# Delta-rule recurrence: inverses merged by 64 x 64 blocks in opposite corners of the array, chunk products kept for the second direction, decays built from stacked rows

## The chip, the cores and the metric

The kernel runs on one core of a Trainium2 chip. The metric is the device time in microseconds, from the launch of the program to its end, of that core. TensorE is called PE in the profile, VectorE DVE, ScalarE ACT, GpSimd POOL and SyncE SP.

## The reference, cut to what matters

The whole program is a two-layer block (two feed-forward networks and a mixer per layer) and then one block with a gated delta rule, a pooling mixer, and an expert-choice feed-forward network. Only the gated delta rule is changed. For each of 4 heads and two directions (forwards, and the sequence reversed) it computes, in chunks:

```python
g = cumsum(log_a)                                   # within a chunk
decay = where(i >= j, exp(g[i] - g[j]), 0)
m = where(i > j, (k*beta) @ k.T * decay, 0)
t_inv = inverse(eye + m)                            # unit lower triangular
w_blk = t_inv @ (k*beta*exp(g));  u_blk = t_inv @ (v*beta)
qk = (q @ k.T) * decay
# scan over the chunks, state s per head and direction:
u_new = u_n - w_n @ s
o_n = (q*exp(g)) @ s + qk @ u_new
s = s * exp(g_last) + (k*exp(g_last - g)).T @ u_new
```

It is computed twice: once for a context of 256 tokens, of which only the final states are wanted (no q), and once for the 512 tokens of the main sequence, which starts from those states.

## The kernel before, in words

The kernel takes chunks of 128 tokens, so the context has 2 and the main sequence 4. A *round* takes one chunk for each direction: round r has chunk r for the forward direction (d = 0) and the last chunk but r for the backward one (d = 1). So the main sequence has 4 rounds and the context 2, and each chunk is met twice, once by each direction. With 4 heads a round has 8 matrices of 128 x 128, m = 4 d + h.

`delta_gates` computes the decays' sums once. `delta_round` is one round up to the inverses, `delta_scan` (L1027) the rest of it. The steps of `delta_round` are:

- *decays*: per direction, two 512-column matmuls (L933, L934) and, for each head, three 128-column ones (L938) whose stationary operands are three parts of the log decay and whose moving operand is a triangle; then exp on ACT (L941) and a product on DVE (L942);
- *chunk products*: keys by keys per direction (L949), times the decays on DVE (L951) and with the diagonal taken out on POOL (L952); the 8 matrices Q go to a scratch tensor in DRAM (L957). In the main sequence also queries by keys (L966, L968);
- *blocks of 16*: the diagonal 16 x 16 blocks are read back, inverted row by row on DVE (L988, L989), and written to two other scratch tensors (L994), which hold zeros elsewhere; these are read back as T and U, 8 whole 128 x 128 matrices each (L999, L1000);
- *merges*: three levels that join blocks of 16, 32 and 64. Each level forms W from Q and T (L1009, copied to SBUF by ACT at L1010), then from W and U the new part of U (L1017) and, in two of the levels, that of T (L1022); a predicated copy on DVE puts the new quarter-blocks in their places (L1023, L1024).

Numbers are fp32; a product of two fp32 operands appears as two rows of 128 columns in the profile, one fp32r product as one row.

The context's rounds run one after the other as side work of the last feed-forward network of layer 1 (`ffn`, whose matmuls are L68 to L70): it takes two steps of the side work after each of its groups of matmuls. The main sequence's rounds are side work of `token_mixer`: its projections of q and v, its pooling mixer (L227 to L229, L1275, L1276, L1285) and its gate projection take 1 to 3 steps after each piece, and a `side.drain()` runs what is left. Two rounds may be open at a time, but a round reads T and U only when the round before has its U (`free`). After the drain the outputs are normalised (L1304 to L1314), turned (L1322) and go through the output projection (`mixer_out`, L68 to L70 again). The instructions are put in order on each engine when the program is built, so parts of the output projection can stand ahead of the last merges; each engine then keeps that order.

Of the kernel before, what the change touches and what calls it, by code (L numbers as in the profile page):

```python
# [11 lines left out]
F32 = mybir.dt.float32  # L12
# [807 lines left out]
def delta_gates(g, ab, nt, pool, pre):  # L820

    nc = g.nc

    def t(n):
        return pool.tile([128, nt, 8], F32, name=pre + n, bufs=1)

    r = {}
    u, la = t("gu"), t("la")
    nc.vector.tensor_add(u, ab[:, :, 0:8], bc(g.V2["dt_bias"][:, None, :], [128, nt, 8]))
    softplus(g, la, u, pool)  # L830
    nc.vector.tensor_mul(la, la, bc(g.V2["negA"][:, None, :], [128, nt, 8]))

    nc.vector.tensor_scalar(la, la, -127.0, None, op0=OP.max)
    be = t("be")
    nc.scalar.activation(be, ab[:, :, 8:16], AF.Exp, scale=-1.0)
    nc.vector.tensor_scalar(be, be, 1.0, None, op0=OP.add)
    nc.vector.reciprocal(be, be)

    a, rest = t("a"), t("rest")
    nc.vector.tensor_scalar(a, la, -786432.0, None, op0=OP.add)  # L840
    nc.vector.tensor_scalar(a, a, 786432.0, None, op0=OP.add)
    nc.vector.tensor_sub(rest, la, a)
    r["parts"] = [pool.tile([128, nt, 8], F32R, name=pre + n, bufs=1) for n in ("pa", "pb", "pc", "pn")]
    nc.vector.tensor_copy(r["parts"][0], a)
    split(g, r["parts"][1], r["parts"][2], rest)
    nc.vector.tensor_scalar(r["parts"][3], a, -1.0, None, op0=OP.mult)
    p = sm(g)
    pv = p[:, :32 * nt].rearrange("p (s a c h) -> p s a c h", s=2, a=2, h=8)
    for i, src in enumerate((a, rest)):
        for d, tri in ((0, g.triu), (1, g.tril)):  # L850
            nc.tensor.matmul(pv[:, 0, i, :, 4 * d:4 * d + 4], tri, src[:, :, 4 * d:4 * d + 4], start=True, stop=True)
        nc.tensor.matmul(pv[:, 1, i], g.ones, src, start=True, stop=True)
    sums = pool.tile([128, 2, 2, nt, 8], F32, name=pre + "sums", bufs=1)
    nc.vector.tensor_copy(sums, pv)

    ex = pool.tile([128, 4, nt, 8], F32, name=pre + "gex", bufs=1)
    nc.vector.tensor_add(ex[:, 0], sums[:, 0, 0], sums[:, 0, 1])
    nc.vector.tensor_sub(sums[:, 0], sums[:, 1], sums[:, 0])
    nc.vector.tensor_add(ex[:, 1], sums[:, 0, 0], sums[:, 0, 1])
    nc.vector.tensor_add(ex[:, 2], sums[:, 1, 0], sums[:, 1, 1])  # L860
    nc.vector.tensor_sub(ex[:, 3], sums[:, 0, 1], sums[:, 1, 1])
    nc.scalar.activation(ex, ex, AF.Exp)
    r["etot"], r["eg"] = ex[:, 2], ex[:, 0]
    r["neg_eg"], r["beta"], r["nbeta"], r["btail"] = t("neg"), t("bex"), t("nbe"), t("bt")
    nc.vector.tensor_scalar(r["neg_eg"], ex[:, 0], -1.0, None, op0=OP.mult)
    nc.vector.tensor_mul(r["btail"], be, ex[:, 1])
    nc.vector.tensor_mul(r["beta"], be, ex[:, 3])
    nc.vector.tensor_scalar(r["nbeta"], r["beta"], -1.0, None, op0=OP.mult)
    r["tri"], r["id"] = g.tri_r, g.id_r
    return r  # L870
# [53 lines left out]
def delta_round(g, cs, kf, gates, P, out, q=None):  # L924
# [4 lines left out]
    e = P["e"]()  # L929
    for d, (tri, mask) in enumerate(gates["tri"]):  # L930
        p = sm(g)
        pa, pb, pc, pn = [t[:, cs[d], 4 * d:4 * d + 4] for t in gates["parts"]]
        nc.tensor.matmul(hv(p), tri, bc(pn[:, :, None], [128, 4, 128]), start=True, stop=False, skip_group_check=True)  # L933
        nc.tensor.matmul(hv(p), gates["id"], bc(mask[:, None, :], [128, 4, 128]), start=False, stop=False,  # L934
                         skip_group_check=True)
        for h in range(4):
            for t in (pa, pb, pc):
                nc.tensor.matmul(p[:, h * 128:(h + 1) * 128], bc(t[:, h:h + 1], [128, 128]), tri, start=False,  # L938
                                 stop=t is pc, skip_group_check=True)
        ed = e[:, 4 * d:4 * d + 4, :]  # L940
        nc.scalar.activation(ed, hv(p), AF.Exp)  # L941
        nc.vector.tensor_mul(ed, ed, bc(gates["nbeta"][:, cs[d], 4 * d:4 * d + 4][:, :, None], [128, 4, 128]))  # L942
        yield
    Q = P["q"]()
    for d in range(2):
        p = sm(g)
        for h in range(4):
            hs = slice(h * 128, (h + 1) * 128)
            nc.tensor.matmul(p[:, hs], kf[cs[d]][:, hs], kf[cs[d]][:, hs], start=True, stop=True)  # L949
        Qd, ed = Q[:, 4 * d:4 * d + 4, :], e[:, 4 * d:4 * d + 4, :]  # L950
        nc.vector.tensor_mul(Qd, ed, hv(p))  # L951
        nc.gpsimd.tensor_mul(Qd, Qd, bc(g.offd[:, None, :], [128, 4, 128]))  # L952
        yield
# [4 lines left out]
    if q is not None:  # L958
        while len(q) < 4:
            yield  # L960
        at = P["at"]()
        for d in range(2):
            p = sm(g)
            for h in range(4):
                hs = slice(h * 128, (h + 1) * 128)
                nc.tensor.matmul(p[:, hs], kf[cs[d]][:, hs], q[h][:, cs[d] * 128:(cs[d] + 1) * 128],  # L966
                                 start=True, stop=True)
            nc.vector.tensor_mul(at[:, 4 * d:4 * d + 4, :], e[:, 4 * d:4 * d + 4, :], hv(p))  # L968
            yield
        out["at"] = at  # L970
# [24 lines left out]
    yield  # L995
    while not P["free"]():
        yield
    T, U = P["t"](), P["u"]()
    nc.sync.dma_start(T, matrices(scr[1]))  # L999
    nc.sync.dma_start(U, matrices(scr[2]))  # L1000
    yield

    for lev in range(3):
        W = P["w"]()
        for d in range(2):
            p = sm(g)
            for h in range(4):
                m = 4 * d + h
                nc.tensor.matmul(p[:, h * 128:(h + 1) * 128], Q[:, m, :], T[:, m, :], start=True, stop=True)  # L1009
            nc.scalar.copy(W[:, 4 * d:4 * d + 4, :], hv(p))  # L1010
        yield
        for d in range(2):
            ds = slice(4 * d, 4 * d + 4)
            pu = sm(g)
            for h in range(4):
                m = 4 * d + h
                nc.tensor.matmul(pu[:, h * 128:(h + 1) * 128], W[:, m, :], U[:, m, :], start=True, stop=True)  # L1017
            if lev < 2:
                p = sm(g)
                for h in range(4):  # L1020
                    m = 4 * d + h
                    nc.tensor.matmul(p[:, h * 128:(h + 1) * 128], U[:, m, :], W[:, m, :], start=True, stop=True)  # L1022
                nc.vector.copy_predicated(T[:, ds, :], bc(g.mrg[:, lev, d, :][:, None, :], [128, 4, 128]), hv(p))  # L1023
            nc.vector.copy_predicated(U[:, ds, :], bc(g.mrg[:, lev, 1 - d, :][:, None, :], [128, 4, 128]), hv(pu))  # L1024
            yield
    out["u"] = U


# [119 lines left out]
def token_mixer(g, I):  # L1148
# [40 lines left out]
    try:  # L1189
        while True:  # L1190
# [10 lines left out]

    spare = [[t, s, t] for t, s in zip([P.tile([128, S], F32, name=f"t_s{d}") for d in range(2)], st)]
    mem.update(at=lambda: P.tile([128, 8, 128], F32, name="t_at", bufs=2),
               u=lambda: P.tile([128, 8, 128], F32, name="t_u", bufs=2), s=lambda d: spare[d].pop())
    res = [{} for _ in range(NT)]
    chunks = [(r, NT - 1 - r) for r in range(NT)]

# [398 lines left out]
def constants():  # L1606
# [17 lines left out]
        "eye16": np.broadcast_to(np.eye(16).reshape(1, 256), (128, 256)),  # L1624
    }
    mrg = []
    for b in (16, 32, 64):
        low = (pc // (2 * b) == q // (2 * b)) & (pc % (2 * b) >= b) & (q % (2 * b) < b)
        mrg += [low, low.T]
    parts["mrg"] = np.concatenate(mrg, 1)  # L1630
    late = ("tril", "mnegb", "offd", "iota", "eye16", "mrg")
    cst, at = [], []
    for names in ([n for n in parts if n not in late], late):
        cst.append(np.ascontiguousarray(np.concatenate([parts[n].astype(np.float32) for n in names], 1)))
# [159 lines left out]
def spread(g, I):  # L1794
# [30 lines left out]
    for i in range(2):  # L1825
        ts = [g.dram.tile([1, 8 * CS], F32, name=f"ds{i}{j}") for j in range(3)]
        for t in ts[1:]:
            for m in (0, 4):
                nc.gpsimd.dma_start(matrices(t)[:, m:m + 4], z)
        g.dscr.append(ts)  # L1830


def setup2(g, I, C):

    g.w_in2 = I["w_in2"]
    _, at, _ = constants()
    cst = C.tile(list(I["cst2"].shape), F32, name="cst2")
    g.nc.scalar.dma_start(cst, I["cst2"])
    for n, sl in at[1].items():
        setattr(g, n, cst[:, sl])  # L1840
    g.mrg = g.mrg.bitcast(I32).rearrange("p (l d c) -> p l d c", l=3, d=2)
    g.s0 = [C.tile([128, S], F32, name=f"s0{d}") for d in range(2)]
    g.wr = C.tile([128, NK, 16], F32, name="wr")
    g.nc.scalar.dma_start(g.wr, I["w_router"].rearrange("(k p) e -> p k e", p=128))

    r = C.tile([128, 5, 128], F32R, name="cst2r")
    for i, src in enumerate((g.triu, g.mneg, g.tril, g.mnegb, g.ident)):
        g.nc.scalar.copy(r[:, i], src)
    g.tri_r, g.id_r = [(r[:, 0], r[:, 1]), (r[:, 2], r[:, 3])], r[:, 4]


def body(tc, I, out):
# [47 lines left out]

# [12 lines left out]
```

## Time and profile before

| | |
|---|---|
| median of 3 runs | 3120.19 us (3111.78 to 3121.61) |
| profiled execution: its time | 3116.74 us |
| profiled execution: span, first to last instruction | 3115.0 us, so 1.7 us lie around it |
| PE busy | 2973.3 us, 95% of the span |
| DVE, ACT, POOL busy | 53%, 29%, 10% |
| mean granted clock of PE | 0.977 of full |
| context's rounds | from 1888 to about 2110 us of the span |
| main sequence's rounds | from 2284 to about 2520 us |

A row of the profile gives a start, a busy time, the engine, the line, the operation, what it writes and reads, and how many instructions the row stands for. Ends of PE rows are modelled, so the price of one in a dense row of them is read from start to start. PEld is the weight load that goes with each matmul.

### The profile page before, as it was taken

The page shows a single profiled execution, that of the slowest core. Times are in us where ns is not written, and L with a number is a line of the kernel's source. Part 1 is how long each engine was busy: PE and PEld are TensorE (multiplying, and loading weights), DVE is VectorE, ACT ScalarE, POOL GpSimd, SP SyncE. Part 2 cuts the span into 40 slices and gives each one's busy share as a digit, 9 for nine tenths or more (in the row PEclk, how much of TensorE's full clock was granted, in tenths as well). Part 3 has the DMA queues.
Part 4 walks back from the last instruction along what each step waited for, and adds up shares of the span by engine and source line. Part 5 has one row for each costly group of instructions (what it writes and reads, how often), then busy time and mean ns, then how long its engine had stood idle before and what let it go on. Part 6 is the DMA issues. An engine that isn't in the chain of part 4 may idle for free. (4 is left out here: it accounts for less than half of the span.)

```text
span 3115.0 us, 37508 instructions
## 1 busy us (share of the span) xinstructions
PE 2973.3 (95%) x15162; PEld 2304.2 (74%) x15162; DVE 1666.3 (53%) x2864; ACT 891.5 (29%) x1442; POOL 319.8 (10%) x250
## 2 busy tenths in 40 slices
PE   7999999999999999999999899999998988999997
PEld 6888888867888888888796788888788876444433
DVE  4445558665445699445776666444764653111213
ACT  3222335333222332223443433222332322000001
POOL 0101012110101102001300201202100011000000
PEclk9999999999999999999999999999999988999998
DMA  4432343122323467224412233222323424999996
GB/s 145 130 98 95 107 141 110 47 70 90 95 95 95 137 215 256 95 94 143 130 53 75 83 108 112 79 86 78 111 70 94 122 109 177 413 417 418 417 419 274
DMA packets 297666, 475.43 MB, mean 153 GB/s; under 512 B 32991, under 2 KB 245727, under 8 KB 275988
## 3 DMA queue, kind: packets, MB, share of 16 engines
q1 hardware_dynamic: 294104, 467.33, 42.8%
q10 hardware_dynamic: 2748, 3.61, 0.4%
q8 instruction: 119, 1.95, 0.3%
q0 software_dynamic: 640, 2.10, 0.3%
q14 instruction: 55, 0.45, 0.0%
HBM read 453.32 MB, written 19.67 MB: 152 GB/s over the span
## 5 line engine op out<-in xcount | busy, mean ns | idle before, releaser
L68 PE MATMUL mm<-xh,whi 128*128 128x512 f32 x1952 | 776.5, 400 | 11.6 <-ACT xh L136 9.0
L69 PE MATMUL mm<-xl,whi 128*128 128x512 f32 x1952 | 771.3, 395 | 0.3 <-DVE xl L40 0.2
L70 PE MATMUL mm<-xh,wlo 128*128 128x512 f32 x1952 | 769.9, 394 | 1.1 <-DVE wlo L40 1.1
L39 ACT CAST whi<-wraw 128x1024 fp32r<-128x1024 f32 (+3 forms) x390 | 390.8, 1003 | 1116.9 <-PE mm L69 869.9
L40 DVE TENSOR_TENSOR wlo<-wraw,whi 128x1024 fp32r<-128x1024 f32 (+3 forms) x390 | 514.2, 1319 | 88.7 <-ACT whi L39 73.3
L68 PEld LDWEIGHTS mm<-xh,whi 128*128 128x128 f32 x1952 | 372.2, 191 | 100.3 <-ACT xh L136 9.9
L69 PEld LDWEIGHTS mm<-xl,whi 128*128 128x128 f32 x1952 | 371.2, 190 | 80.1 <-issue 2.5
L70 PEld LDWEIGHTS mm<-xh,wlo 128*128 128x128 f32 x1952 | 371.0, 190 | 77.8 <-DVE wlo L40 1.9
L68 PE MATMUL mm<-hh,whi 128*128 128x512 f32 x704 | 278.8, 396 | 0.0
L70 PE MATMUL mm<-hh,wlo 128*128 128x512 f32 x704 | 277.9, 395 | 0.0
L69 PE MATMUL mm<-hl,whi 128*128 128x512 f32 x704 | 276.1, 392 | 0.0
L182 POOL TENSOR_TENSOR x<-x,dt 128x512 f32<-128x512 f32 x72 | 116.1, 1613 | 945.3 <-DVE dt L181 925.6
L162 DVE TENSOR_TENSOR gs<-mm,rb 128x512 f32<-128x512 f32 x88 | 60.7, 690 | 212.1 <-PE mm L70 207.8
L181 DVE SCALAR_TENSOR_TENSOR dt<-mm,rb 128x512 f32<-128x512 f32 x104 | 71.8, 690 | 173.5 <-PE mm L70 173.3
L167 DVE TENSOR_TENSOR gs<-gs,mm 128x512 f32<-128x512 f32 x88 | 60.4, 686 | 193.3 <-PE mm L70 193.2
L70 PEld LDWEIGHTS mm<-hh,wlo 128*128 128x128 f32 x704 | 132.2, 188 | 30.7
L69 PEld LDWEIGHTS mm<-hl,whi 128*128 128x128 f32 x704 | 132.2, 188 | 30.4 <-DVE hl L40 0.3
L68 PEld LDWEIGHTS mm<-hh,whi 128*128 128x128 f32 x704 | 132.3, 188 | 28.2
L227 PE MATMUL mm<-whi,xh 128*128 128x256 f32 (+1 forms) x448 | 131.5, 293 | 0.0
L229 PE MATMUL mm<-whi,xl 128*128 128x256 f32 (+1 forms) x448 | 128.8, 287 | 0.0
L228 PE MATMUL mm<-wlo,xh 128*128 128x256 f32 (+1 forms) x448 | 128.5, 287 | 0.0
L1521 PE MATMUL mm<-e_raw,e_x 128*64 128x512 f32 x536 | 123.1, 599 | 3.8 <-DMA e_raw<-e_up 2.7
(615 smaller groups left out, 3858.6 us busy)
## 6 DMA issues: line engine op xcount, KB each, us to landing
e_raw<-e_down SPq DMA_DIRECT2D x45, 1024.0 KB, 13.8
wraw<-ffn_gate SPq DMA_DIRECT2D x44, 1024.0 KB, 5.4
wraw<-ffn_up SPq DMA_DIRECT2D x44, 1024.0 KB, 5.4
e_raw<-e_up SPq DMA_DIRECT2D x41, 1024.0 KB, 15.0
wraw<-w_in SPq DMA_DIRECT2D x38, 1024.0 KB, 5.3
e_raw<-e_gate SPq DMA_DIRECT2D x26, 1024.0 KB, 12.6
wraw<-ffn_down SPq DMA_DIRECT2D x24, 1024.0 KB, 5.0
mw<-w_mod SPq DMA_DIRECT2D x24, 1024.0 KB, 5.1
```

The lines of the kernel that those rows point to most:

```text
L39: g.nc.scalar.copy(hi, src)
L40: g.nc.vector.tensor_sub(lo, src, f32(hi))
L68: g.nc.tensor.matmul(out, lh, rh, start=(i == 0), stop=False)
L69: g.nc.tensor.matmul(out, lh, rl, start=False, stop=False)
L70: g.nc.tensor.matmul(out, ll, rh, start=False, stop=(i == n - 1))
L162: nc.vector.tensor_mul(gs, pg, rb)
L181: nc.vector.scalar_tensor_tensor(t, pd, 0.25, rb, op0=OP.mult, op1=OP.mult)
L182: (nc.vector if c0 + nch == sum(groups) else nc.gpsimd).tensor_add(g.x[2 * c + m], g.x[2 * c + m], t)
L227: nc.tensor.matmul(o, xh[:, kk, ts], wh, start=(kk == 0), stop=False)
L228: nc.tensor.matmul(o, xh[:, kk, ts], wl, start=False, stop=False)
L229: nc.tensor.matmul(o, xl[:, kk, ts], wh, start=False, stop=(kk == NK - 1))
L1521: nc.tensor.matmul(ps[h][pj[j], :], lhs(k, j), raw[j][:, h * 512:(h + 1) * 512], start=(k == 0), stop=(k == NK - 1), skip_group_check=True)
```

## The change

Five things are changed, all of them in or around `delta_gates` and `delta_round`.

1. *Merges.* T, V (the former U) and W hold only the two diagonal 64 x 64 blocks of each matrix, so they are [128, 8, 64]. The levels of 16 and 32 are done on these: for each matrix one matmul on rows and columns 0 to 63 of the array and one on rows and columns 64 to 127 (`blocks`), all 16 into one PSUM tile. The level of 64 is one 64 x 64 block per matrix, two matmuls each, and the result is copied into U, whose other corner is set to zero by POOL. T and V come from DRAM in two half-partition reads each.
2. *Chunk products* are kept in the main sequence: the first direction that meets a chunk copies the product from PSUM to a kept SBUF tile, the other reads that tile. In the context they are computed each time, as before.
3. *Decays*: the cumulative sums are split in hi and lo, stacked and turned once in `delta_gates` into rows; in `delta_round` each head then takes two matmuls with a constant selector in place of three.
4. The zeros of the scratch tensors are written by SP's queue, not POOL's, and the program reserves 1024 bytes of scratch for dynamic DMA.
5. The masks for the predicated copies are 64 columns wide and there are two levels of them.

```diff
@@ delta_gates
-    r["parts"] = [pool.tile([128, nt, 8], F32R, name=pre + n, bufs=1) for n in ("pa", "pb", "pc", "pn")]
-    nc.vector.tensor_copy(r["parts"][0], a)
-    split(g, r["parts"][1], r["parts"][2], rest)
-    nc.vector.tensor_scalar(r["parts"][3], a, -1.0, None, op0=OP.mult)
+    r["na"] = pool.tile([128, nt, 8], F32R, name=pre + "pn", bufs=1)
+    nc.vector.tensor_scalar(r["na"], a, -1.0, None, op0=OP.mult)
...
+    parts = pool.tile([128, nt, 4, 8], F32R, name=pre + "parts", bufs=1)
+    for i in range(2):
+        split(g, parts[:, :, 2 * i], parts[:, :, 2 * i + 1], sums[:, 0, i])
+    rows = r["rows"] = pool.tile([128, nt * 128], F32R, name=pre + "rw", bufs=1)
+    nc.gpsimd.memset(f32(rows), 0.0)
+    pt = sm(g)
+    for i in range(nt):
+        nc.tensor.transpose(pt[0:32, i * 128:(i + 1) * 128], f32(parts[:, i]).rearrange("p a b -> p (a b)"), g.ident)
+    nc.scalar.copy(rows[0:32, :], pt[0:32, :nt * 128])
@@ delta_round
-            for t in (pa, pb, pc):
-                nc.tensor.matmul(p[:, h * 128:(h + 1) * 128], bc(t[:, h:h + 1], [128, 128]), tri, start=False,
-                                 stop=t is pc, skip_group_check=True)
+            for i in range(2):
+                m = 8 * i + 4 * d + h
+                nc.tensor.matmul(p[:, h * 128:(h + 1) * 128], bc(g.stkd_r[:, m:m + 1], [128, 128]),
+                                 gates["rows"][:, cs[d] * 128:(cs[d] + 1) * 128], start=False, stop=i == 1,
+                                 skip_group_check=True)
...
+    def inner(name, c, rhs):
+        kept = P.get("kept")
+        if kept is not None and (name, c) in kept:
+            return kept[name, c]
+        p = sm(g)
         for h in range(4):
             hs = slice(h * 128, (h + 1) * 128)
-            nc.tensor.matmul(p[:, hs], kf[cs[d]][:, hs], kf[cs[d]][:, hs], start=True, stop=True)
+            nc.tensor.matmul(p[:, hs], kf[c][:, hs], rhs(h, hs), start=True, stop=True)
+        if kept is None:
+            return p
+        t = kept[name, c] = P["keep"]()
+        nc.scalar.copy(t, p)
+        return t
...
-    T, U = P["t"](), P["u"]()
-    nc.sync.dma_start(T, matrices(scr[1]))
-    nc.sync.dma_start(U, matrices(scr[2]))
+    halves = [slice(0, 64), slice(64, 128)]
+    T, U, W = P["t"](), P["u"](), P["w"]()[:, :, 0:64]
+    T, V = T[:, :, 0:64], T[:, :, 64:128]
+    for t, dst in ((1, T), (2, V)):
+        for r, hf in enumerate(halves):
+            nc.sync.dma_start(dst[hf], matrices(scr[t])[hf, :, hf])
+    for d in range(2):
+        nc.gpsimd.memset(U[halves[1 - d], 4 * d:4 * d + 4, halves[d]], 0.0)
     yield
-    for lev in range(3):
...
+    def blocks(lhs, rhs):
+        p = sm(g).rearrange("p (m c) -> p m c", m=8)
+        for m in range(8):
+            for hf in halves:
+                nc.tensor.matmul(p[hf, m, :], lhs(hf, m), rhs[hf, m, :], start=True, stop=True, skip_group_check=True)
+        return p
+
+    for lev in range(2):
+        nc.scalar.copy(W, blocks(lambda hf, m: Q[hf, m, hf], T))
+        yield
+        pu = blocks(lambda hf, m: W[hf, m, :], V)
+        p = blocks(lambda hf, m: V[hf, m, :], W)
         for d in range(2):
             ds = slice(4 * d, 4 * d + 4)
...
+            for dst, src, i in ((T, p, d), (V, pu, 1 - d)):
+                nc.vector.copy_predicated(dst[:, ds, :], bc(g.mrg[:, lev, i, :][:, None, :], [128, 4, 64]), src[:, ds, :])
+        yield
+
+    p = sm(g)[:, 0:256].rearrange("p (h c) -> p h c", h=4)
+    for h in range(4):
+        for d in range(2):
+            c, a = halves[d], halves[1 - d]
+            nc.tensor.matmul(p[a, h, :], Q[c, 4 * d + h, a], T[c, 4 * d + h, :], start=True, stop=True,
+                             skip_group_check=True)
+    nc.vector.tensor_copy(W[:, 0:4, :], p)
+    for hf, copy in zip(halves, (nc.scalar.copy, nc.gpsimd.tensor_copy)):
+        copy(U[hf, :, hf], V[hf])
+    yield
+    p = sm(g)[:, 0:256].rearrange("p (h c) -> p h c", h=4)
+    for h in range(4):
+        for d in range(2):
+            c, a = halves[d], halves[1 - d]
+            nc.tensor.matmul(p[c, h, :], W[a, h, :], V[a, 4 * d + h, :], start=True, stop=True, skip_group_check=True)
+    for d in range(2):
+        (nc.scalar.copy if d else nc.vector.tensor_copy)(U[halves[d], 4 * d:4 * d + 4, halves[1 - d]], p[halves[d]])
+    yield
     out["u"] = U
@@ spread
-                nc.gpsimd.dma_start(matrices(t)[:, m:m + 4], z)
+                nc.sync.dma_start(matrices(t)[:, m:m + 4], z)
@@ kernel
-    nc = bacc.Bacc("TRN2", target_bir_lowering=False, num_devices=1)
+    nc = bacc.Bacc("TRN2", target_bir_lowering=False, num_devices=1, dynamic_dma_scratch_size=1024)
```

## Rows read from the trace of the kernel before

**Rows 1.** Windows: length, busy us of PE, PEld, DVE, ACT, POOL, granted clock, DMA.
```profile
1780.00:2200.00 420.00, 415.66 (x2148) 351.76 (x2147) 234.82 (x397) 119.88 (x173) 51.32 (x31) 1.00 0.31 94
2280.00:2489.00 209.00, 194.33 (x1410) 181.45 (x1408) 126.14 (x301) 64.00 (x104) 11.64 (x11) 0.97 0.36 101
2489.00:2520.00 31.00, 30.10 (x260) 29.45 (x260) 19.67 (x49) 6.53 (x12) 0.00 (x0) 1.00 0.10 35
```

**Rows 2.** Who PE waited for, 1780 to 2535 us: total, times, longest.
```profile
PE sm L1009 <- DMA x<-ds: 9.6, 4, 3.4
PE sm L1009 <- DMA c<-ds: 3.8, 1, 3.8
PE sm L1009 <- DVE x L1023: 0.3, 1, 0.3
```

**Rows 3.** Groups by line on PE, main sequence (4 rounds).
```profile
L1017 PE MATMUL sm<-t_u,x 128*128 128x128 f32 x192 | 25.5, 278 | 0.0
L1022 PE MATMUL sm<-x,t_u 128*128 128x128 f32 x128 | 16.9, 275 | 0.0
L938 PE MATMUL sm<-cst2r,t_pa 128*128 128x128 f32 x32 | 8.4, 261 | 0.0
L949 PE MATMUL sm<-t_kf 128*128 128x128 f32 x64 | 8.4, 276 | 0.0
```

**Rows 4.** Timeline of PE in a dense stretch of merges and decays.
```profile
2402.12 1.06 PE L1022 MATMUL sm<-x,t_u 128*128 128x128 f32 x8
2403.01 1.06 PE L1017 MATMUL sm<-t_u,x 128*128 128x128 f32 x8
...
2405.24 0.22 PE L938 MATMUL sm<-cst2r,t_pa 128*128 128x128 f32 x1
...
2406.53 0.32 PE L1009 MATMUL sm<-x 128*128 128x128 f32 x1
```

**Rows 5.** Timeline of PE: one 512-column fp32 product on the whole array.
```profile
62.49 1.02 PE L1816 MATMUL sm<-bflip,cst 128*128 128x512 f32 x2
```

**Rows 6.** By line: ns of one row, min/median/max, first and last start.
```profile
L1521 PE MATMUL mm<-e_raw,e_x x536: 592/592/643, 2620.7 to 3039.1; 128*64 128x512 f32 x179
L1376 PE MATMUL sm<-cst,e_full x4: 201/208/208, 2608.9 to 2609.1; 16*128 16x16 f32 x4
```

**Rows 7.** Timeline of PE in the experts: matmuls on halves of the columns.
```profile
2659.98 1.89 PE L1521 MATMUL mm<-wraw,e_x 128*64 128x512 f32 x8
2661.80 0.66 PE L1533 MATMUL sm<-cst,e_hs 128*128 128x128 f32 x4
2662.39 1.08 PE L1521 MATMUL mm<-wraw,e_x 128*64 128x512 f32 x4
```

**Rows 8.** Timeline: small matmuls on quarters of the columns.
```profile
1171.75 0.16 PEld L780 LDWEIGHTS sm<-mr,mfold 128*32 128x32 f32 x8 [0.36 <-issue]
```

**Rows 9.** Timeline of PE: small matmuls one after the other, in one place.
```profile
2608.94 0.39 PE L1376 MATMUL sm<-cst,e_full 16*128 16x16 f32 x4 [1.60 <-DVE e_full L1372]
```

**Rows 10.** Groups by line on DVE and ACT, main sequence.
```profile
L1024 DVE COPY_PREDICATED t_u<-cst,sm 128x512 f32<-128x512 int32 x24 | 17.3, 722 | 2.0 <-PE sm L1017 2.0
L1297 DVE SCALAR_TENSOR_TENSOR t_b<-t_scr,t_b 128x256 f32<-128x256 f32 x8 | 3.6, 446 | 2.7 <-ACT t_b L1296 2.7
L1010 ACT COPY x<-sm 128x512 f32<-128x512 f32 x24 | 14.1, 587 | 52.3 <-PE sm L1009 52.3
```

**Rows 11.** DMA issues, 2280 to 2535 us: KB each, us to landing.
```profile
x<-ds SPq DMA_DIRECT2D x4, 512.0 KB, 5.7
t_u<-ds SPq DMA_DIRECT2D x4, 512.0 KB, 7.6
```

**Rows 12.** Timeline of SP: the read of T in a round.
```profile
2366.03 0.52 SPq L999 DMA_DIRECT2D x<-ds  x1
```

**Rows 13.** Timeline of PE: after a read of T, and at the mixer's end.
```profile
2371.53 3.17 PE L1009 MATMUL sm<-x 128*128 128x128 f32 x16 [3.35 <-DMA x<-ds]
...
2528.37 1.11 PE L1322 MATMUL sm<-cst,t_raw 128*128 128x128 f32 x4 [8.81 <-POOL t_raw L1314]
```

More of the change, by code (lines that the diff above doesn't have):

```diff
@@ L931, in delta_round @@
         p = sm(g)
-        pa, pb, pc, pn = [t[:, cs[d], 4 * d:4 * d + 4] for t in gates["parts"]]
+        pn = gates["na"][:, cs[d], 4 * d:4 * d + 4]
         nc.tensor.matmul(hv(p), tri, bc(pn[:, :, None], [128, 4, 128]), start=True, stop=False, skip_group_check=True)
@@ L944, in delta_round @@
     Q = P["q"]()
-    for d in range(2):
+    def inner(name, c, rhs):
+        kept = P.get("kept")
+        if kept is not None and (name, c) in kept:
+            return kept[name, c]
         p = sm(g)
@@ L948, in delta_round @@
             hs = slice(h * 128, (h + 1) * 128)
-            nc.tensor.matmul(p[:, hs], kf[cs[d]][:, hs], kf[cs[d]][:, hs], start=True, stop=True)
+            nc.tensor.matmul(p[:, hs], kf[c][:, hs], rhs(h, hs), start=True, stop=True)
[5 more added lines that the diff above has]
+    for d in range(2):
+        c = cs[d]
+        p = inner("k", c, lambda h, hs: kf[c][:, hs])
         Qd, ed = Q[:, 4 * d:4 * d + 4, :], e[:, 4 * d:4 * d + 4, :]
@@ L962, in delta_round @@
         for d in range(2):
[L963 to L967, printed above, removed]
+            c = cs[d]
+            p = inner("q", c, lambda h, hs: q[h][:, c * 128:(c + 1) * 128])
             nc.vector.tensor_mul(at[:, 4 * d:4 * d + 4, :], e[:, 4 * d:4 * d + 4, :], hv(p))
@@ L997, in delta_round @@
         yield
-    T, U = P["t"](), P["u"]()
-    nc.sync.dma_start(T, matrices(scr[1]))
-    nc.sync.dma_start(U, matrices(scr[2]))
-    yield
-    for lev in range(3):
[L1004 to L1010, printed above, removed]
+    halves = [slice(0, 64), slice(64, 128)]
@@ L1011, in delta_round @@
+    for lev in range(2):
+        nc.scalar.copy(W, blocks(lambda hf, m: Q[hf, m, hf], T))
         yield
+        pu = blocks(lambda hf, m: W[hf, m, :], V)
+        p = blocks(lambda hf, m: V[hf, m, :], W)
         for d in range(2):
             ds = slice(4 * d, 4 * d + 4)
[L1014 to L1023, printed above, removed]
@@ L1024, in delta_round @@
-            nc.vector.copy_predicated(U[:, ds, :], bc(g.mrg[:, lev, 1 - d, :][:, None, :], [128, 4, 128]), hv(pu))
-            yield
+            for dst, src, i in ((T, p, d), (V, pu, 1 - d)):
[7 more added lines that the diff above has]
+                             skip_group_check=True)
@@ new lines, in delta_round @@
+    nc.vector.tensor_copy(W[:, 0:4, :], p)
[7 more added lines that the diff above has]
+            nc.tensor.matmul(p[c, h, :], W[a, h, :], V[a, 4 * d + h, :], start=True, stop=True, skip_group_check=True)
+    for d in range(2):
+        (nc.scalar.copy if d else nc.vector.tensor_copy)(U[halves[d], 4 * d:4 * d + 4, halves[1 - d]], p[halves[d]])
@@ L1203, in token_mixer @@
     mem.update(at=lambda: P.tile([128, 8, 128], F32, name="t_at", bufs=2),
-               u=lambda: P.tile([128, 8, 128], F32, name="t_u", bufs=2), s=lambda d: spare[d].pop())
+               u=lambda: P.tile([128, 8, 128], F32, name="t_u", bufs=2), s=lambda d: spare[d].pop(),
+               kept={}, keep=lambda: P.tile([128, S], F32, name="t_keep", bufs=8))
     res = [{} for _ in range(NT)]
@@ L1626, in constants @@
     mrg = []
-    for b in (16, 32, 64):
+    for b in (16, 32):
         low = (pc // (2 * b) == q // (2 * b)) & (pc % (2 * b) >= b) & (q % (2 * b) < b)
-        mrg += [low, low.T]
+        mrg += [np.tile(m[:64, :64], (2, 1)) for m in (low, low.T)]
     parts["mrg"] = np.concatenate(mrg, 1)
-    late = ("tril", "mnegb", "offd", "iota", "eye16", "mrg")
+    parts["stkd"] = np.concatenate([(pc // 16 == i) & (pc % 8 == np.arange(8)[None, :]) for i in range(2)], 1)
+    late = ("tril", "mnegb", "offd", "iota", "eye16", "mrg", "stkd")
     cst, at = [], []
@@ L1840, in setup2 @@
         setattr(g, n, cst[:, sl])
-    g.mrg = g.mrg.bitcast(I32).rearrange("p (l d c) -> p l d c", l=3, d=2)
+    g.mrg = g.mrg.bitcast(I32).rearrange("p (l d c) -> p l d c", l=2, d=2)
     g.s0 = [C.tile([128, S], F32, name=f"s0{d}") for d in range(2)]
@@ L1844, in setup2 @@
     g.nc.scalar.dma_start(g.wr, I["w_router"].rearrange("(k p) e -> p k e", p=128))
[L1846 to L1849, printed above, removed]
+    r = C.tile([128, 5 * 128 + 16], F32R, name="cst2r")
+    srcs = (g.triu, g.mneg, g.tril, g.mnegb, g.ident)
+    for i, src in enumerate(srcs):
+        g.nc.scalar.copy(r[:, i * 128:(i + 1) * 128], src)
+    g.stkd_r = r[:, 640:656]
+    g.nc.scalar.copy(g.stkd_r, g.stkd)
+    r = [r[:, i * 128:(i + 1) * 128] for i in range(5)]
+    g.tri_r, g.id_r = [(r[0], r[1]), (r[2], r[3])], r[4]
 def body(tc, I, out):
```

## Prediction, made before the changed kernel ran

> **What bounds the kernel now.** I read the page first: PE is busy 95% of the span, no other engine over 53%. Then the windows around the two places where the rounds run. In the context's part the feed-forward network keeps PE busy 415.66 of 420 us, and in the main sequence's 194.33 of 209 us and then 30.10 of the last 31 us [rows 1]. So in both places PE's own work sets the end, and a PE row taken out is worth about what it takes. Third, the waits: PE idles before the first matmul of the merges for the read of T, 9.6 us in four times and 3.8 us once, but only 0.3 us for the predicated copies [rows 2]; the chains of the merges are covered by other work today. Fourth, the groups by line, for how many rows each step has, and last the timeline, for what one costs: eight rows of 128 columns take 2403.01 - 2402.12 = 0.89 us, 0.111 us each [rows 4]. (Their modelled durations, 0.275 us [rows 3], overlap and are no price.)
>
> **Merges.** Before, L1017 has 192 rows and L1022 128 in the four main rounds [rows 3]; L1009, formed at the same three levels as L1017, has 192 too. That is 512 / 4 = 128 rows a round, 128 x 0.111 = 14.2 us; six rounds make 85 us.
>
> After, a round has 2 levels x 3 products x 16 blocks + 2 x 8 = 112 products, 224 rows, of 64 columns on 64 of 64. More rows, so all depends on what one takes. No row of this trace has blocks in opposite corners. The lower bound: half the columns halve 0.111 to 0.056, and if the two corners run at once, two rows share that: 0.028 us a row. That two parts of the array do run at once is what the experts show. A 512-column fp32 product on the whole array has its two rows 1.02 - 0.59 = 0.43 us apart, 0.59 being one row's modelled length [rows 5, 6], but on halves of the columns eight rows last 1.89 us: four pairs, (1.89 - 0.59) / 3 = 0.43 us from pair to pair [rows 7]. So each pair takes what one row takes. Small ones can follow closely too: eight weight loads on four quarters of the columns last 0.16 us in all [rows 8]. The upper bounds: 0.060 us, from the only rows of small matmuls one after the other in one place, (0.39 - 0.21) / 3 [rows 6, 9]; and 0.111 if a small row costs what a large one does. I take 0.033, near the pairs of [rows 7, 8], which also alternate between parts of the array, with a little for short rows: 224 x 0.033 = 7.4 us.
>
> The Trainium skill, TensorE: Matmul & The Clock Gate, section Back-to-back issue gap, speaks against so low a price: for 64 columns or fewer it gives a floor of about 25 ns a matmul, but about 62 ns where the sequencer's firmware decodes. By the first the 0.028 stands; by the second 224 rows would take an estimated 13.9 us and the merges would gain nothing. The burst of [rows 8] is too short to decide it.
>
> To this comes the change from the whole array to parts of it and back. In [rows 7] the transposes start 0.09 us later than another pair would (2661.80 against 2659.98 + 1.89 - 0.59 + 0.43), the pair after them 0.09 us later than a fifth transpose would, and the first rows on each side lag by 0.06 us: 0.30 us for there and back. A round has six such groups (two for each of three levels): 1.8 us if other work stands between all of them. So 7.4 + 1.8 = 9.2 us against 14.2: -5.0 us a round, -30 us in all. Bounds: -48 us (0.028, no changes of tile), +6 us (0.060), +75 us (0.111).
>
> **Decays.** Three matmuls a head become two. Twelve take 2406.53 - 2405.24 = 1.29 us, 0.108 each [rows 4]. L938 has 32 rows for each of its three parts in four rounds [rows 3], so 48 for one part in six: -5.2 us. The six transposes added to `delta_gates` are at most 0.111 each, +0.7 us. Its further splits and copies on ACT and DVE, and one memset on POOL, come nine side steps before the first use.
>
> **Chunk products.** L949 has 64 rows [rows 3], L966 as many. In the main sequence half of both go: 64 x 0.111 = -7.1 us. Eight copies of 0.59 us [rows 10] are added on ACT, which is busy 64 of 209 us there [rows 1]: nothing, but in the first two rounds the product on DVE starts that much later, behind a copy. Without that room on ACT they would cost 4.7 us.
>
> **The chains.** A level was worked in two halves, one per direction, so that one half's copy ran beside the other's matmuls. Now one copy of 0.59 us stands between W and what follows, and four predicated copies of 256 columns behind that. Before they were 0.72 us each at 512 columns; 0.45 us is the nearest row of 256 columns [rows 10]. That is 0.59 + 4 x 0.45 = 2.4 us a level and, for two more copies of 256 columns, twice 0.45 in the last: 5.7 us a round in which PE needs other work. In the context the network's matmuls give it. In the main sequence the other round, the scan and the projections do, as far as their order allows: between 0 and 4 x 5.7 = 23 us are open. I take +4, near the 0.3 us that the copies cost today [rows 2], since a round takes three side steps fewer: counting steps in the code, eleven are left for the drain before, two after, so more of the rounds stand beside the gate projection. POOL's copy of half of U's blocks runs beside the last level.
>
> **Costed at nothing.** T and V are read in four DMAs of half a block's width, half the bytes, in place of two. Each further issue is about 0.5 us on SP [rows 12]. T lands 5.7 us after issue, U 7.6 [rows 11]. PE waits for T, and T's two reads are first, so what is late is V's, which the second step needs. If nothing covered it, two more issues x 6 rounds = 6 us. The eight writes of zeros go to SP's queue while the first feed-forward network runs; SP waits there for buffers, not the other way. The wait for T's read stays in all five places, and after one PE runs at its lower clock: 16 rows take 3.17 us [rows 13] where 0.111 each would be 1.8.
>
> **Sum.** -30 - 5.2 + 0.7 - 7.1 + 4 = -38 us. From the profiled execution's 3116.74 us that is 3079 us. That execution is 3.4 us under the median of the runs shown, so for a median I say 3080 us. About 0.3%, 9.4 us, is what a measurement can tell from no change.
>
> **Rivals.**
> - *Small rows cost as much as large ones* (the corners don't share time, and loads aren't hidden): 0.111 us each, +75 - 5 + 1 - 7 + 4: 3184 us, slower. For it speaks that every 128-column row here has that price whatever its type, fp32 or fp32r [rows 4]; against it the pairs of [rows 7]. It decides from 0.061 us a row: 224 x 0.061 + 1.8 is the 14.2 us of before and 1.3 us, a sixth of what the other edits bring net. Slower by over 0.3% from 0.068 us.
> - *A floor of 0.060 us a row* [rows 9], because each small matmul has to be issued: +6 - 12 + 4, 3115 us, no change. For it speaks that 28 ns must hold over 64 rows at a stretch; against it the burst of [rows 8], and that PE's queue fills while 512-column matmuls run. It is the mechanism of the skill's 62 ns.
> - *The main rounds become a chain.* All 23 us of copies lie open in place of 4: 3098 us. For it speaks that only 0.9 us in 31 are idle in the last stretch [rows 1], so there is no slack there; against it the fewer steps left for the drain.
> - *More than I say.* 0.028 us a row, no changes of tile, and the 8.8 us in which PE waits for the outputs' normalisation at the mixer's end [rows 13] filled with output projection: -48 - 12 - 9, about 3048 us.
>
> **How the numbers follow.** Chances: my forecast (25 to 55 us saved) 0.52, more 0.10, chain 0.13, floor 0.15, slower 0.10. Range 3052 to 3114 us: between the last rival and the floor; the slow rival is left out. The forecast's own range is 3062 to 3092. Faster by over 0.3%: 0.52 + 0.10 + 0.13 and a little of the floor, 0.78. Within: 0.12. Slower: 0.10.
>
> **What would show it.** 224 rows of 64 columns a round in the merges; their starts in pairs a few ns apart and about 0.06 us from pair to pair. If pairs are 0.12 us apart, the floor is right; at 0.22 the slow rival. L949 and L966 with 32 rows each in the main sequence, two rows a head in the decays. The context's stretch shorter by some 12 us, the main one by some 26. What would make it wrong: the price of a small row, first of all; then idle time of PE before the second product of a level.

## The result, and the profile after

The changed kernel took 3079.96 us (median of four runs, 3075.28 to 3084.72) beside 3117.21 us for the kernel before (four runs): ratio 0.9878, 95% interval 0.9859 to 0.9896. A second measurement gave 3072.09 us, 0.9853 (0.9835 to 0.9872). The forecast was 3080 us. The profiled execution took 3075.28 us, its span is 3073.4.

The stages show where this came from. Their bounds are the first row of the modulation ahead of the context's part, the same row ahead of the main mixer, the first turning transpose at the mixer's end, and the end of the span. Lengths in us, one profile each:

| kernel | start | context's part | main mixer | rest (router, experts) |
|---|---|---|---|---|
| before | 1776.1 | 445.2 | 307.1 | 586.6 |
| changed | 1775.5 | 431.0 | 286.9 | 580.0 |
| changed, second profile | 1773.2 | 428.4 | 289.2 | 581.3 |

The context's part lost 14 to 17 us (forecast 12), the main mixer 18 to 20 (forecast 26), and the rest 5 to 7, of which the forecast had nothing. The start shows nothing of the change (the zeros on SP's queue, the shorter constants): it lasts 1771.8 to 1781.6 us in three profiles of the kernel before (two of them with one small edit, below) and 1773.2 to 1775.5 in three of the changed one.

Windows of the changed kernel (length, busy us of PE, PEld, DVE, ACT, POOL, granted clock of PE as a share of full, DMA share, GB/s); the first is that of [rows 1], the next two are the two stages, the last is the main mixer of the second profile:

```profile
1780.00:2200.00 420.00, 414.34 (x2375) 343.68 (x2374) 244.99 (x410) 124.29 (x180) 59.15 (x44) 0.99 0.33 99
1775.40:2206.50 431.10, 421.58 (x2406) 349.77 (x2404) 252.28 (x432) 127.33 (x187) 59.45 (x45) 0.99 0.32 97
2206.50:2493.40 286.90, 254.54 (x2248) 222.21 (x2248) 191.93 (x477) 98.46 (x164) 21.16 (x20) 0.94 0.31 85
2201.60:2490.80 289.20, 255.79 (x2248) 223.40 (x2248) 191.94 (x477) 98.45 (x164) 20.98 (x20) 0.92 0.30 84
```

The context is as dense as before, so what PE no longer does there is gained whole. In the main mixer PE is busy for 254.54 us of 286.90. The same stage of the kernel before:

```profile
2221.30:2528.40 307.10, 282.44 (x1957) 257.12 (x1957) 199.35 (x476) 99.18 (x162) 12.90 (x12) 0.96 0.30 86
```

PE's busy time fell by 27.9 us, the stage by 20.2: idle time grew from 24.7 to 32.4 us, and the granted clock fell from 0.96 to 0.94.

Groups by line on PE in the main mixer of the changed kernel, which answer to [rows 3]:

```profile
L1036 PE MATMUL sm<-x 64*64 64x64 f32 x768 | 27.9, 224 | 12.8 <-DMA x<-ds 10.3 <-ACT x L1040 1.4 <-DVE x L1047 1.0
L948 PE MATMUL sm<-t_rw,cst2r 128*128 128x128 f32 x64 | 8.4, 274 | 0.0
L965 PE MATMUL sm<-t_q,t_kf 128*128 128x128 f32 x32 | 4.4, 275 | 0.0
L965 PE MATMUL sm<-t_kf 128*128 128x128 f32 x32 | 3.9, 276 | 0.0
L1054 PE MATMUL sm<-x 64*64 64x64 f32 x64 | 3.4, 226 | 1.3 <-DVE x L1047 1.3
L1064 PE MATMUL sm<-x 64*64 64x64 f32 x64 | 2.8, 226 | 0.6 <-DVE x L1056 0.6
```

The counts are those forecast: (768 + 64 + 64) / 4 = 224 rows a round, 32 rows for each kind of chunk product, two decay rows a head. What one takes is read from the timeline of PE in the context, whole array, blocks, whole array:

```profile
1951.04 0.40 PE L70 MATMUL mm<-xh,wlo 128*128 128x512 f32 x1
1951.28 0.39 PE L68 MATMUL mm<-xh,whi 128*128 128x512 f32 x1
1951.60 2.08 PE L1036 MATMUL sm<-c 64*64 64x64 f32 x64
1953.61 0.50 PE L69 MATMUL mm<-xl,whi 128*128 128x512 f32 x1
```

From the first block to the next large row are 2.01 us for 64 rows, 0.031 a row with both changes of tile partly in it. Inside, the starts come in pairs 6 or 7 ns apart and 58 ns from pair to pair (read from the single starts in the trace): 0.029 us a row, held over 64 rows.

### The profile page after: what moved, and what is told of

Read it like the earlier page. It is cut to its first block, busy times and chain, and to the rows that moved or that the text cites. A ratio compares the mean times of both kernels' runs of the same rounds, so it can differ in the third digit from the quotient of the medians.

```text
span 3073.4 us, 38461 instructions
## 1 busy us (share of the span) xinstructions
PE 2929.7 (95%) x15632; PEld 2251.2 (73%) x15632; DVE 1655.6 (54%) x2864; ACT 888.6 (29%) x1443; POOL 324.7 (11%) x262
```

## The experiments

All comparisons are with the kernel before on the same chip, five rounds each.

**Which part brought the time.** Three variants take parts of the change out again. The first keeps only the merges; the second leaves out the kept products, the third has the old decays.

```
-   mem.update(..., kept={}, keep=lambda: P.tile([128, S], F32, name="t_keep", bufs=8))
+   mem.update(...)                                      # first and second variant
-   for i in range(2): ... g.stkd_r[:, m:m + 1] ... gates["rows"] ...
+   for t in (pa, pb, pc): ... bc(t[:, h:h + 1], ...) ... tri ...     # first and third
```

> The changed kernel with the three-product decays of before and without kept chunk products: the merges are the only part left. The prediction's sum: merges -30, chains +4, so some 26 us below the kernel before (ratio 0.992). The sum with the merge rows resized from the changed kernel's trace (-13.6 in the context, -25.3 in the main rounds on TensorE) and the idle time that grew there: -28 to -35 (0.989 to 0.991). Rival, the merges give all and the 12 us of the two other parts disappear in waits: -37 (0.988), as fast as the whole change.

> The changed kernel, but each direction computes its own chunk products in the main rounds. Theory (the prediction's term): 64 more rows of 0.111 us, +7.1 us against the changed kernel, ratio to before about 0.990. Rival: the main rounds have about 32 us of idle TensorE and are chains there, so the 7 us fall into it and the ratio stays 0.988; kept products also cost 8 copies of ScalarE, so a small gain from leaving them out is possible in that case.

> The changed kernel with three products a head for the decays as before, in context and main. Theory (the prediction's terms): +5.2 for 48 more rows, -0.7 for the transposes that go, so +4.5 us against the changed kernel, ratio to before about 0.989. Rival: hidden in waits, ratio 0.988 with no difference that can be measured.

Measured: 3078.43 us, ratio 0.9889 (0.9872 to 0.9906); 3079.52 us, 0.9883 (0.9867 to 0.9899); 3079.11 us, 0.9886 (0.9869 to 0.9902). So the merges alone bring most of it. Pooled, the two measurements of the whole change lie at 0.9866, and the 0.9889 of the merges alone is some 7 us above with as much uncertainty: these times don't say how much of the 11.6 us of the other two parts arrived. The stages say a little more. Context and main mixer together last 714.7 to 717.9 us in three profiles of the changed kernel (the third is the one with a shifted buffer, below), 725.0 without kept products, 720.2 with the old decays, and 721.2 without both. One by one they are worth about what the forecast said (8 and 3 us, for 7.1 and 4.5); together only 4.5. These differences are hardly above the scatter: the three profiles of the changed kernel differ by 3.2 us among themselves, and the one without kept products is of that kernel's slowest run, 3.9 us above its median. The main mixer without both:

```profile
2204.90:2494.10 289.20, 262.94 (x2340) 232.36 (x2340) 188.64 (x476) 93.56 (x154) 18.02 (x20) 0.94 0.30 84
```

PE is busy for 8.4 us more than in the changed kernel, and idle for 6 less. Rows that are taken out of the main mixer turn partly into idle time.

**Do the opposite corners share time?** The same blocks, one corner after the other:

```
-    for m in range(8):
-        for hf in halves:
+    for hf in halves:
+        for m in range(8):
```

and the same exchange of the two loops at the level of 64.

> The changed kernel with the same quarter blocks, but all of one corner first and then all of the other, instead of in turn; the same rows, operands and results. Theory (two corners are worked on at once, so a pair of rows costs what one costs alone): a row starts 0.058 us after the one before instead of 0.029, 224 rows a round x 0.029 = +6.5 us a round, +39 us over six rounds if TensorE bounds all of them, +13 for the context alone if the main rounds hide theirs: ratio to before between 0.992 and 1.000. Rival (the rate depends on the columns of a row alone): rows 0.029 us apart in either order, ratio 0.988.

Measured: 3115.19 us, ratio 1.000 (0.9983 to 1.0017). The order of the blocks is worth the whole gain. The timeline in the context:

```profile
1960.45 0.40 PE L68 MATMUL mm<-xh,whi 128*128 128x512 f32 x1
1960.78 3.40 PE L1036 MATMUL sm<-c 64*64 64x64 f32 x64
```

64 rows last 3.40 us instead of 2.08, and in one corner each row starts 58 ns after the one before (at a change of corner two rows still overlap). Over all groups of merges, from the first block to the next other row, PE takes 24.5 us in the context and 63.7 in the main rounds, against 15.7 and 36.0 in the changed kernel: 36.5 us more, and by the ratios the whole takes (1.000 - 0.9878) x 3117 = 38 us more. So TensorE's own time is what counts in both stages, for merges too.

Not all of the 36.5 us is the rows' price, though. In the context the granted clock was 0.99 in both kernels, and there the exchange costs 8.8 us for 448 rows; by that, the 896 rows of the main rounds would cost an estimated 18 us. They cost 27.7, because in this run's main mixer the clock was 0.88 and stood at its lower level, 0.50 (1.2 GHz), for 41 us on end. The main mixer, that stretch of it, and 64 rows in it:

```profile
2221.80:2537.70 315.90, 285.20 (x2248) 253.22 (x2248) 192.67 (x476) 98.50 (x164) 20.48 (x20) 0.88 0.28 77
2349.40:2390.40 41.00, 31.10 (x273) 29.44 (x272) 15.37 (x52) 3.44 (x8) 1.62 (x4) 0.50 0.14 34
2350.89 6.29 PE L1036 MATMUL sm<-x 64*64 64x64 f32 x64 [0.68 <-ACT x L1040]
```

That two corners share time is thus read from the context; by this estimate some 10 of the 36.5 us are granted clock. Why the clock fell there for so long no run shows.

**What PE waits for in the main mixer.** Waits of the changed kernel there (total, times, longest):

```profile
PE sm L1036 <- DMA x<-ds: 10.3, 3, 6.4
PE mm L1328 <- DVE t_scr L1324: 7.8, 2, 7.6
PE mm L1328 <- DMA t_pw<-pool_w: 3.1, 1, 3.1
PE sm L1365 <- POOL t_raw L1357: 3.2, 1, 3.2
PE sm L1036 <- ACT x L1040: 1.4, 2, 0.7
PE sm L1054 <- DVE x L1047: 1.3, 2, 1.1
```

L1328 is the pool_w product, which in the kernel before (L1285) waited 3.6 us:

```profile
PE mm L1285 <- DVE t_scr L1281: 3.3, 2, 2.3
PE mm L1285 <- DVE t_scr L988: 0.3, 1, 0.3
```

The long wait in the changed kernel, on PE and on DVE:

```profile
2404.02 0.39 PE L1319 MATMUL mm<-whi,t_b 128*128 128x512 f32 x1
2411.99 2.07 PE L1328 MATMUL mm<-t_scr,t_pw 128*128 128x512 f32 x2 [7.58 <-DVE t_scr L1324]
2413.08 1.42 PE L1318 MATMUL mm<-whi,t_b 128*128 128x512 f32 x1
```

```profile
2408.48 1.21 DVE L40 TENSOR_TENSOR wlo<-wraw,whi 128x1024 fp32r<-128x1024 f32 x1
2409.61 1.42 DVE L1010 TENSOR_TENSOR t_scr<-dl_X,dl_D 64x121 f32<-64x121 f32 x1
2411.07 0.27 DVE L1011 TENSOR_REDUCE dl_X<-t_scr 64x11 f32<-64x121 f32 x1
2411.26 0.67 DVE L1324 TENSOR_TENSOR t_scr<-mm,t_scr 128x512 f32<-128x512 f32 x1
```

The factor ahead of the product stands in DVE's queue behind decays, a weight split and the substitution of a later round. And the longest wait for T's read:

```profile
2344.66 3.59 PE L1081 MATMUL sm<-s,t_kf 128*128 128x128 f32 x16
2354.64 0.44 PE L1036 MATMUL sm<-x 64*64 64x64 f32 x2 [6.39 <-DMA x<-ds]
2355.01 1.65 PE L1081 MATMUL sm<-t_scr,t_u 128*128 128x128 f32 x6
```

The scan's products (L1081) stand behind the block product that waits, in PE's queue; what they need was on DVE until 2349.7 and then ready:

```profile
2348.09 1.63 DVE L1087 SCALAR_TENSOR_TENSOR t_scr<-sm,t_neg,t_vt 128x128 f32<-128x128 f32 x6
```

Two edits try to use these waits, one more step behind T's reads, and the pump moved ahead of the pool_w product with its tile loaded one turn earlier:

```
     yield
+    if q is not None:
+        yield
```

```
+            side.pump(2)
             p = g.ps_m.tile([128, 512], F32, name="mm")
             nc.tensor.matmul(p, pw, m, start=True, stop=True)
             nc.scalar.activation(yp[:, q, :], p, ...)
-            side.pump(2)
```

> The changed kernel with one more step in the main rounds, right behind the DMA reads of T and V, so that the scan of the round before issues its products before the first quarter-block product that needs these reads. Theory (TensorE stands at those products because nothing else is issued ahead of them): the three waits of 10.3 us in all, longest 6.4, are filled with scan products, 4 to 8 us less than the changed kernel, ratio to before 0.985 to 0.987. Rival (the recurrence is a chain of steps, and an extra step per round is paid at the end, where nothing else is left): the wait goes and 2 to 8 us come back in the last stretch of the mixer, ratio 0.988 to 0.990.

> The changed kernel with two edits around the pool_w product: two recurrence steps are issued before that product instead of after it, and the pool_w tile is loaded one turn ahead. Theory (TensorE stands at that product for VectorE, 7.8 us, and for the tile's DMA, 3.1 us, with recurrence work ready behind it): 6 to 11 us less than the changed kernel, ratio to before 0.984 to 0.986. Rival (what is put in the gap waits for the same VectorE or for T's read itself, so the idle time moves on): ratio 0.988, as the changed kernel, with the waits at other lines.

> The changed kernel with both edits: the extra step behind T's reads and the two steps ahead of the pool_w product with its tile loaded ahead. If both theories hold, 10 to 19 us less than the changed kernel, ratio to before 0.982 to 0.985; if the idle time only moves, 0.987 to 0.990.

Measured: 0.9879 (0.9863 to 0.9894), 0.9868 (0.9848 to 0.9888) and 0.9872 (0.9859 to 0.9885); in us 3079.30, 3079.12 and 3077.74. None can be told from the changed kernel. The main mixer lasts 292.3, 282.9 and 291.4 us. With the extra step, and then with the pump moved, its waits are

```profile
PE mm L1330 <- DVE t_scr L1326: 15.9, 2, 11.4
PE sm L1038 <- DMA x<-ds: 6.6, 3, 4.2
```

```profile
PE sm L1036 <- DMA x<-ds: 8.9, 2, 6.3
PE mm L1333 <- DVE t_scr L1326: 8.3, 2, 7.6
```

The step took 3.7 us from the read's waits, and the pool_w product waits 15.9 us in place of 7.8 + 3.1: the rival, by which idle time moves on, holds for it. Of the pump's edit only the tile's early load shows, the 3.1 us are gone; the wait for VectorE is 8.3 us instead of 7.8, so other rows put ahead on PE did not shorten it, as one expects where DVE's queue is what is late. No run changes DVE's order, so that it sets this wait is read from the rows above and not tested.

**The experts' 6 us.** No instruction of the experts changed. The transfers are at their limit there, with a DMA share of 1.01 to 1.02, and PE, busy for 98 of 100 us, still waits for `e_raw` in the last stage: 10.0 us before and 6.6 after. The expert weights moved at 417 to 418 GB/s before and 422 to 423 after, and the last stage is at 580 to 582 us in all variants so far, even in the one that is as slow as before. Two things that the change sets could do it. One is the DMA scratch, put into the kernel before by itself:

```
-    nc = bacc.Bacc("TRN2", target_bir_lowering=False, num_devices=1)
+    nc = bacc.Bacc("TRN2", target_bir_lowering=False, num_devices=1, dynamic_dma_scratch_size=1024)
```

> The kernel before with one edit, the size of the DMA scratch that the change also sets. In the changed kernel and its four variants so far the stretch from the first turning transpose to the end is 580 to 582 us, in the one profile of before 586.3. Theory: the scratch has nothing to do with it and the 586.3 is that execution's own; ratio 1.000, and a second profile of this code shows 580 to 586. Rival: the scratch's size gives these 5 us: ratio 0.9985, stretch 581.

Measured: ratio 1.000 (0.9989 to 1.0012), last stage 586.4 us. Not the scratch. (The expectations count the last stage from its second group of rows, 0.3 us later than the tables here.) The other is where the buffers lie. The changed constants are 1920 bytes a partition shorter, and in the built program the seven buffers of `e_raw`, 8192 bytes a partition each, begin on a multiple of 512 bytes, where before they began 384 behind one. An unused tile behind the constants moves them, and all other buffers behind the constants with them:

```
     setup2(g, I, c2)
+    c2.tile([128, 96], F32, name="pad2")     # changed kernel: 384 bytes
+    c2.tile([128, 32], F32, name="pad2")     # kernel before: 128 bytes
```

> The changed kernel with an unused tile of 384 bytes a partition behind the constants, so that the seven expert weight buffers (e_raw) begin where they begin in the kernel before: 384 bytes behind a multiple of 512, instead of on one. Theory (the 5.5 us that the experts lost, with DMA at its limit there and 423 GB/s instead of 417, come from that place and from nothing in the recurrence): the stretch from the first turning transpose to the end goes from 579.8 back to about 586, the rate to 417 GB/s, ratio to before about 0.9895. Rival (the experts gain from something else, such as other queues or the smaller constants): 580 to 582 us, 423 GB/s, ratio 0.988.

> The kernel before with an unused tile of 128 bytes a partition behind the constants, so that the expert weight buffers begin on a multiple of 512 bytes. Theory (place alone): the last stretch goes from 586.3 to about 580.5, the rate from 417 to 423 GB/s, everything ahead of it as before: ratio 0.998. Rival: 586 us, 1.000.

> The changed kernel once more, beside the others: the stages of a second profile say how far one execution's stages can be told apart, and five more rounds say whether the merges alone (0.9889) are slower than the whole. By the prediction's terms the whole is 11.6 us below the merges alone (0.985 to 0.986), by the rival (the rest is lost in waits) the same (0.988).

One window of 100 us in the experts, each from its own kernel's profile; before, and before on the multiple of 512:

```profile
2798.00:2898.00 100.00, 98.47 (x485) 42.13 (x483) 23.45 (x39) 7.59 (x13) 0.00 (x0) 1.00 1.02 417
```

```profile
2804.00:2904.00 100.00, 98.46 (x485) 42.18 (x485) 23.07 (x39) 7.09 (x12) 0.00 (x0) 1.00 1.02 422
```

The changed kernel, and the changed kernel shifted by 384 bytes:

```profile
2763.00:2863.00 100.00, 98.47 (x485) 42.26 (x484) 23.45 (x39) 7.42 (x13) 0.00 (x0) 1.00 1.02 422
```

```profile
2759.00:2859.00 100.00, 98.47 (x487) 42.18 (x484) 23.45 (x39) 7.48 (x13) 0.00 (x0) 1.00 1.02 417
```

The last stage follows the place in both kernels: 585.9 us for the changed kernel when shifted (580.0 and 581.3 unshifted), 582.1 for the kernel before on the multiple (586.6 and 586.4). In times: the kernel before becomes 0.9984 (0.9973 to 0.9994); the changed kernel is 3079.15 us, 0.9878 (0.9861 to 0.9894) when shifted, and 3072.09, 0.9853 (0.9835 to 0.9872), unshifted beside it; the two intervals overlap, so of the changed kernel only the stage and the rate tell. That it is the place of `e_raw`, and not that of another buffer behind the constants, is inferred from the rate of its transfers.

**All weight buffers in place, and the pump moved.** 480 bytes ahead of `wraw`, `whi` and `wlo` put `wraw` on multiples of 512 and the other two on multiples of 256, and 32 bytes behind the constants leave `e_raw` on a multiple of 512. The pump is moved as above, without the early load of the tile:

> The changed kernel with 480 bytes ahead of the weight buffers wraw, whi and wlo and 32 behind the constants, so that all of them and e_raw begin on multiples of 256 or 512 bytes, and with two recurrence steps issued ahead of each pool_w product (without the early load of its tile). If the place of wraw, whi and wlo costs the experts as that of e_raw does, the last stretch falls by a further 1 to 3 us; with 4 us from the order of the steps, ratio to before 0.985 to 0.987. If their place does not count and the idle time moves on, 0.988.

Measured: 3071.56 us, 0.9854 (0.9835 to 0.9874), against 3072.09 for the changed kernel beside it: no difference in time. In the profile the last stage is 578.8 us, the lowest of all, at 424 to 425 GB/s; the main mixer lasts 285.2 us.

## Why the prediction was right, and where it was not

The sum was -38 us. By the ratio the first measurement is -38 (0.0122 x 3117.21), the second -46, both pooled -42. The stages give -36 without the experts (means over the changed kernel's profiles: context 429.1, main 287.6, against 445.1 and 307.3 over three of the kernel before) and some -6 in the experts, together about the same. So the mechanism and the total are right, but that the total comes so close is in part luck: the merges with their waits gave some 32 us (31 by the stages of the variant with the merges alone) where the terms had 26, the other two parts together perhaps 4.5 where they had 11.6, and the experts' 6 were in no term.

- *The price of a small row*, on which all depended, was 0.033 and is 0.029 us; the corners share time, which the exchange of their order shows: 2.08 against 3.40 us for 64 rows in the context. No floor of 60 ns a row: 64 rows in a run kept 29 ns each. Of the two figures of the Trainium skill (TensorE: Matmul & The Clock Gate, section Back-to-back issue gap) 62 ns a row is excluded here, and 25 ns is left; counted by product, two rows each, the run gives 58 ns, just under 62.
- *The change of tile* was 0.30 us there and back. Start to start it is 0.32: the first block comes 0.08 us late, the second pair 0.05, and the next two large rows 0.09 and 0.10.
- *The merges* were to bring -30 us. From the first block to the next other row, the groups fell from 29.3 to 15.7 us in the context and from 61.3 to 36.0 in the main rounds: -39 us. This leaves out what lies outside a group, its late first block and the late second large row behind it, 0.18 us together. There are 24 groups in the main rounds and 13 in the context, six or a little more a round as forecast, so 6.7 us come back: -32 us, and -36 without the waits inside the groups. A round cost 14.6 to 15.3 us before, where the forecast counted 14.2, and after the change 9.0 to 9.2 without waits, the 9.2 forecast. The old rows were the dearer ones: some ran at the lower clock, 16 of them in 3.17 us [rows 13], which the price of 0.111 leaves out.
- *The chains* were to cost +4 us. PE's waits for copies inside the merges in the main mixer are 1.4 + 1.3 + 1.0 + 0.6 = 4.3 us in place of 0.3 [rows 2]: the term holds in size; its reason, the fewer steps left for the drain, was not tested. The rival of all 23 us did not come.
- *What was lost in the main mixer* is the step that failed: there a row taken out was not worth what it takes. By price, 24.3 us of merges (61.0 against 36.7, without waits and with the changes of tile), 3.5 of decays, 7.1 of chunk products, less 0.4 of transposes, PE had 34.5 us less to do; its busy time fell by 27.9. The granted clock, 0.96 before, 0.94 and 0.92 in the two profiles after, makes most of that difference of 6.6 us: PE was busy at the lower level, 0.50, for 17 us before and for 28 and 32 us after, and half of that is lost, an estimated 8.5 us before and 14.2 and 15.9 after. After the 7.58 us wait the pool_w product's two rows last 2.07 us, where a pair of that size was 1.02 [rows 5]. Another 7.7 us became idle time, 4 of them the chains, 7.3 the pool_w product, while the wait at the mixer's end [rows 13] fell. The prediction followed the merges' own waits and not DVE's queue, which other rows of the projections share.
- *The wait for T's read* did not stay in five places; it stands in three in the main mixer, for 10.3 us as against 9.6 [rows 2], and in one in the context, for 2.2.
- *Place of the weight buffers*: 5 to 6 us that no step had. It made up for what the main mixer lost.
- *From the profiled execution to the median* the sum goes up by 1 us, though it names 3.4; the difference is below what these measurements can tell.

Open: how much is left of the kept products and new decays together (4.5 us by the stages of one profile, 0 to 14 by the times).

## What to carry to other kernels

Two quarter blocks in opposite corners, issued in turn, cost what one costs; the same blocks sorted by corner, with the clock that this order cost, gave all of it back. In the stage that was full, a row removed was time gained; where other queues stand close behind, look at what PE will wait for next, because a long wait can also cost clock. And before a small gain in a transfer-bound stage is put down to an edit, see whether the edit moved the buffers.

## What the runs showed of the hardware

- 64 x 64 blocks of fp32 with 64 columns: 58 ns from row to row in one corner, 58 ns from pair to pair in two opposite ones issued in turn, both at a granted clock of 1.00.
- With the blocks sorted by corner, the granted clock stood at 0.50 for 41 us of the main mixer, in which PE was busy for 31.1 us; with the corners in turn, the two longest waits, 6.4 and 7.6 us, each have 6.8 us at 0.50 at their end and behind them. Why the first lasts so long is not shown.
- Going from rows on the whole array to such blocks and back costs about 0.32 us.
- Expert weights land at 422 to 423 GB/s in buffers that begin on a multiple of 512 bytes of the partition and at 417 to 418 where they begin 384 bytes behind one: 1.3%, in both kernels and both directions. The Trainium skill (DMA: Bandwidth & Descriptors, section How a descriptor splits into AXI transactions) has a descriptor that does not begin on a multiple of 256 bytes start its first transaction at the multiple below, with bytes fetched and not used; 384 is no such multiple. The direction agrees, but the page states it of reads and these are the places written to, and no run here tries another remainder of `e_raw`: why is not shown.
